# ScalarE and VectorE in program order through the whole attention part of a decoder layer, and other queues and turns for three of its steps

## The chip, the cores and the metric

The kernel runs on one core of one Trainium2 chip. The metric is device time in microseconds (us), the median of several runs of the same program; smaller is better. The profile is that of one execution. Engines go by the profile's names: PE multiplies matrices, DVE (VectorE) and ACT (ScalarE) do element-wise work, POOL and SP here mainly issue transfers. PSUM is the memory that PE writes; a 128x512 float32 tile of it is called a bank here.

## The reference, cut to what matters

One decoder layer for 512 tokens of width 1024, all in float32:

```python
h = RMSNorm(x);  z = h @ w_in            # one projection, cut into the parts below
A  = retention(rq, rk, rv)               # 4 heads, group norm, silu(rg) gate, @ w_ret_out
for (window, dilation) in (128,1), (512,4), (2048,16):   # 3 head groups, 4 heads of 128 each
    q, k = rotate(RMSNorm(aq)), rotate(RMSNorm(ak))
    s = q k^T / sqrt(128), masked;  m = max(s);  e = exp(s - m);  l = sum(e)
    o_g = (e / l) v;  lse_g = m + log(l)
Bt = sum_g softmax_g(lse_g) * o_g        # groups merged by their denominators, @ w_att_out
x  = x + (sig(gA) * A' + sig(gB) * Bt') @ w_o
x  = x + relu(RMSNorm(x) @ w_up)^2 @ w_down
x  = x + sig(RMSNorm(x) @ w_pg) * (p @ w_pp)
```

The change lies in the three groups of the attention. With 512 tokens, group 0 has four blocks of 128 queries, three of them with 256 keys; groups 1 and 2 have four blocks of 128 queries and 128 keys each, groups 1 and 2 being gathered by residue classes of the token number.

## The kernel before, in words

**Products.** Every product of two float32 matrices is made of three matmuls of a shorter type: each operand is split into a high part and the rest. For a weight, a piece of 128x1024 is loaded (`raw`, L212, by SP), ACT writes its high part (`whi`, L250), DVE the rest (`wlo`, L251), and `mm3` (L262 to L264) issues three matmuls on PE. `whi` and `wlo` have four buffers each, `raw` six. Units of weights are fetched and split two ahead of their use (`ahead`, `units`).

**Seven products.** The projections of the values, of the retention's keys and a few more are made by `seven_products`, which saves one of eight block products: sums of loaded weights are made by DVE (`raw<-raw,raw`, L226) or on the way in by POOL's accumulating DMA (L228). Its results leave PSUM by `after` in `values_seven`: products 1, 3, 4 and 5 by ACT's copy (L757), 2, 6 and 7 by DVE (L759, L761), which adds the bank to what stands in SBUF (`m`, `v`). A bank (`pg`, `pa`, `sc`, `pe`, `ph`, `po`, `pc` are its names) takes the next product only once it was read.

**Attention.** `att_proj` makes q or k of a group and rotates it (L575 to L580), with the norm's factor from POOL (L651) applied at L655; `scores` multiplies q and k to a bank `sc`, and `softmax` takes it: DVE adds the mask (`sm`, L678), takes the maximum (`mx`, L681) and the bias (`st`, L682, L684), ACT takes the exponential and its sum (`se`, L687). `turn` transposes the exponentials on PE (`pe`, L694), `weigh_values` multiplies them with the values (`po`, L835). `rescale` merges a group with those before it: factors `f`, `w`, `inv` (L863 to L871), for the last group the scaling of its sixteen exponential tiles by ACT (`se`, L876), `wide` (L878) and its transposition on PE (`pc`, L884), through DRAM to all partitions (L887, L892) and onto the output `oT` (L897).

**Order.** The Python program writes instructions in one order: a product, and between its pieces what stands in a queue of deferred steps (`later(lag, ...)` at the end, `prompt(lag, ...)` at the front; a lag is counted in pieces, `tick`; `force` runs the queue until a named step is done). A scheduler then fixes the order on each engine and may move instructions ahead of one another. Inside `manual_schedule(engines=...)` the named engines keep the written order. Before the change that held in the attention for the first two projections only (L703); outside it the scheduler chose.

Of the kernel before, what the change touches and what calls it, by code (L numbers as in the profile page):

```python
# [11 lines left out]
F32 = mybir.dt.float32  # L12
# [5 lines left out]
P = 128  # L18
S = 512
D = 1024  # L20
NT = S // P
# [3 lines left out]
H = 4  # L25
HD = 128
NG = 3
DIL = 4
# [51 lines left out]
class Block:  # L80
# [618 lines left out]
    def attention(self):  # L699

        nc = self.nc
        with self.tc.manual_schedule(engines={nc.scalar.engine, nc.vector.engine}):
            qk = self.att_proj(0, 0), self.att_proj(0, 1)  # L703
        nc.sync.dma_start(self.mask, self.a["c_mask"])
        self.gain_rows(1, NG)
        self.rot_rows(1)
        self.spare = True
        self.left = self.token_factors_seven()
        rq = self.rq
        qk1 = self.att_proj(1, 0), self.att_proj(1, 1)  # L710
        pT = [self.big("pT") for _ in range(2)]
        first, turned = self.scores(0, *qk, rq, None, pT)
        strided = self.const.tile([P, NT, 2, H], F32, name="st0p")
        self.prompt(10, lambda: self.to_strided(first, strided))
        past, turned1 = self.scores(1, *qk1, self.rq, strided, None, 18)
        self.later(24, lambda: self.rescale(1, strided, past), ("past", 1))
        v0, v1 = self.values_seven((self.r, self.r_minus))
        for g, v, pTs, lag in ((0, v0, turned, 2), (1, v1, turned1, 8)):
            values = self.weigh_values(g, v, pTs)
            for r in range(NT):  # L720
                self.later(lag, lambda r=r, values=values: values(r), ("att", g, r))
        qk = self.att_proj(2, 0), self.att_proj(2, 1)
        last, turned = self.scores(2, *qk, self.rq, past, None, 14)
        self.later(21, lambda: self.rescale(2, past, last), ("past", 2))
        dec, kdec = self.decays()
        kd, v2 = self.values_seven((None, self.r_minus), self.ret_keys(kdec))
        values = self.weigh_values(2, v2, turned)
        for r in range(NT):
            self.later(5, lambda r=r, values=values: values(r), ("att", 2, r))
        return dec, kd  # L730

    def values_seven(self, scale, ready=None):

        nc = self.nc
        for j in range(2):
            self.force(("S", j))
        held, out = {}, {}

        def tile(n):
            if n not in out:  # L740
                out[n] = self.big("v")
            return out[n]

        def after(m, p, ps):
            t = p if m in (1, 2, 3, 6) else 2 + p
            main = m in (1, 2, 4)
            r = scale[0 if main else 1]
            by = {} if r is None else dict(scale=r[:, t : t + 1])
            if main:
                o = tile(0)[:, t]  # L750
            elif m in (3, 5):
                o = self.tmp("m3") if m == 3 else self.tabp.tile([P, 512], F32, tag="tab", name=self.nm("m5"))
                held[{3: 6, 5: 7}[m], p] = o
            else:
                o = held.pop((m, p))
            if m in (1, 3, 5, 4):
                nc.scalar.activation(o, ps, AF.Copy, **by)  # L757
            elif r is None:
                nc.vector.tensor_tensor(o, o, ps, op=ALU.add)  # L759
            else:  # L760
                nc.vector.scalar_tensor_tensor(o, ps, r[:, t : t + 1], o, op0=ALU.mult, op1=ALU.add)  # L761
            if m in (6, 7):
                for q in range(DIL):
                    nc.sync.dma_start(tile(1)[32 * t : 32 * (t + 1), q], o[q : P : DIL])
            if m in (2, 4) and ready is not None:
                ready(t, o)

        self.seven_products(self.left, after)
        return tile(0), tile(1)

    def scores(self, g, qT, kT, rq, past, held=None, lag=2):

        nc = self.nc
        st = self.const.tile([P, NT, 2, H], F32, name=f"st{g}")
        pTs = [[] for _ in range(NT)]
        self.es = {}
        slots = None if held is None else [b[:, i] for b in held for i in range(4)]

        def block(r):
            m, l = st[:, r, 0], st[:, r, 1]  # L780
            rs = slice(r * P, (r + 1) * P)
            es = []
            wide = g == 0 and r > 0
            if not wide:
                sc = self.bank("sc")
                for h in range(H):
                    nc.tensor.matmul(sc[:, h * P : (h + 1) * P], qT[:, h, rs], kT[:, h, rs], start=True, stop=True)  # L787
                es.append(self.softmax(sc, P, H, self.mask[:, 128 * (g + 1) : 128 * (g + 2)], rq[:, r], m, l,
                                       None if past is None else past[:, r, 0]))
                self.es[g, r] = es[0]  # L790
            else:
                for hp in range(2):
                    sc = self.bank("sc")
                    for h in range(2):
                        nc.tensor.matmul(sc[:, h * 256 : (h + 1) * 256], qT[:, 2 * hp + h, rs],
                                         kT[:, 2 * hp + h, (r - 1) * P : (r + 1) * P], start=True, stop=True)
                    hs = slice(2 * hp, 2 * hp + 2)
                    es.append(self.softmax(sc, 256, 2, self.mask[:, 0:256], rq[:, r, hs], m[:, hs], l[:, hs]))
            for e in es:
                self.later((5, 8, 11)[g], lambda e=e: turn(e, r), ("pT", g, r))  # L800

        def turn(e, r):
            if g == 2:
                self.force(("past", 2))
            if g == 1 and not self.pT1:
                self.pT1.append(self.big("pT"))
            out = slots.pop(0) if slots else self.pT1[0][:, r] if g == 1 else None
            pTs[r].append(self.transpose4(e, out))

        for r in range(NT):  # L810
            self.later(lag, lambda r=r: block(r), ("sc", g, r))
        return st, pTs
# [43 lines left out]
    def rescale(self, g, past, st):  # L856
# [25 lines left out]
        def turn():  # L882
            ps = self.bank("pc")
            nc.tensor.transpose(ps[: H * NT, :P], wide, self.ident)  # L884
            turned = self.turned[: H * NT]
            nc.scalar.activation(turned, ps[: H * NT, :P], AF.Copy)
            nc.scalar.dma_start(d.rearrange("a (r l) -> (a r) l", r=DIL), turned)  # L887
# [4 lines left out]
                nc.scalar.dma_start(spread[0][:, h], d[h : h + 1].to_broadcast([P, S]))  # L892

        def scale():
            for h in range(H):
                o = self.oT[0][:, h]
                nc.vector.tensor_tensor(o, o, spread[0][:, h], op=ALU.mult)  # L897
# [619 lines left out]
```

## Time and profile before

| | before |
|---|---|
| runs | 954.59, 952.70, 952.63 us |
| median | 952.7 us |
| the profiled execution, time | 955.36 us |
| its span on the core | 953.6 us, so 1.8 us lie around it |
| mean granted PE clock | 0.997 |
| PE busy | 943.3 us, 99% of the span |
| DVE busy | 718.4 us, 75% |
| ACT busy | 562.1 us, 59% |
| POOL busy | 159.5 us, 17% |

The attention part lies between about 70 and 270 us of the span: the first group's softmaxes at 105 to 119 us, the second's at 135 to 146 us, the third's at 239 to 250 us. In rows of the profile, `out<-in` names the tiles that an instruction writes and reads; a time in brackets at a row's end is how long the engine idled before it, and for whom. Matmuls of PE overlap, so the time between two starts, not a row's duration, is what one costs.

### The profile page before, as it was taken

Reading aid. Unit: us, or ns where it says so; the run is one execution under the profiler, and the core shown is the slowest. Engines: PE = TensorE matmul, PEld = TensorE weight load, DVE = VectorE, ACT = ScalarE, POOL = GpSimd, SP = SyncE. Lnnn points to the kernel's source line nnn. Section 1 sums busy time; section 2 is a strip of 40 time slices with the busy share of each in tenths; the row PEclk is TensorE's granted clock in tenths of the full one; section 3 lists DMA queues with packets and bytes.
Section 4 is the critical chain, followed back from the end, with each engine's and each line's share of the span. In section 5 each row is a group of like instructions: output and inputs, shape, how many; then the busy total and the mean of one; then the engine's idle time right before and its main releaser. Section 6 shows DMA issues by size and latency. Waiting matters only on the chain.

```text
span 953.6 us, 14325 instructions
## 1 busy us (share of the span) xinstructions
PE 943.3 (99%) x5357; PEld 826.2 (87%) x5357; DVE 718.4 (75%) x997; ACT 562.1 (59%) x1065; POOL 159.5 (17%) x140
## 2 busy tenths in 40 slices
PE   9999999999899999999999999999999999999998
PEld 6888888888788888999988888988998998998887
DVE  7789964766697849386937889799499689769953
ACT  5657775445745566576714446884494486467651
POOL 0322210222001112223012211111212302112100
PEclk9999999999999999999999999999999999999999
DMA  9953466258437645869737677868958968876911
GB/s 333 282 170 82 106 141 215 64 118 195 148 111 155 173 100 138 163 181 217 232 115 236 148 178 214 206 153 222 199 156 202 191 183 157 224 172 159 288 50 56
DMA packets 92549, 162.87 MB, mean 171 GB/s; under 512 B 8608, under 2 KB 20544, under 8 KB 92480
## 3 DMA queue, kind: packets, MB, share of 16 engines
q1 hardware_dynamic: 65168, 113.37, 36.4%
q0 software_dynamic: 23936, 46.14, 29.0%
q10 hardware_dynamic: 3376, 2.44, 0.9%
q8 instruction: 42, 0.69, 0.3%
q14 instruction: 27, 0.22, 0.1%
HBM read 153.49 MB, written 6.34 MB: 168 GB/s over the span
## 4 chain that ended last, share of the span: by engine, by line
PE 92%; DVE 3%; ACT 1%; issue 1%; DMA 1%; POOL 1%; SPq 0%; ACTq 0%; POOLq 0%; DVEq 0%
PE pg L264 25%; PE pg L262 25%; PE pg L263 25%; PE pa L264 3%; PE pa L263 3%; PE pa L262 3%; PE po L835 1%; PE ph L590 1%; DVE wlo L251 1%; PE pe L694 1%; PE sc L787 1%; PE ry L1083 1%; PE kv L1070 1%; PE ry L1085 1%; DVE ro L578 0%
## 5 line engine op out<-in xcount | busy, mean ns | idle before, releaser
L251 DVE TENSOR_TENSOR wlo<-raw,whi 128x1024 fp32r<-128x1024 f32 (+1 forms) x258 | 306.8, 1198 | 112.7 <-ACT whi L250 111.8
L250 ACT ACTIVATE whi<-raw 128x1024 fp32r<-128x1024 f32 (+1 forms) x257 | 266.3, 1041 | 212.1 <-PE pg L264 87.2
L263 PE MATMUL pg<-f,whi 128*128 128x256 f32 x384 | 108.7, 283 | 0.0
L264 PE MATMUL pg<-f,wlo 128*128 128x256 f32 x384 | 108.7, 283 | 0.0
L262 PE MATMUL pg<-f,whi 128*128 128x256 f32 x384 | 108.7, 283 | 0.0
L262 PE MATMUL pg<-whi,hh 128*128 128x512 f32 x248 | 98.6, 398 | 0.0
L264 PE MATMUL pg<-whi,hl 128*128 128x512 f32 x248 | 97.1, 392 | 0.0
L263 PE MATMUL pg<-wlo,hh 128*128 128x512 f32 x248 | 96.8, 390 | 0.0
L262 PE MATMUL pg<-whi,f 128*128 128x512 f32 x192 | 75.4, 393 | 0.0
L263 PE MATMUL pg<-wlo,f 128*128 128x512 f32 x192 | 74.8, 389 | 0.0
L264 PE MATMUL pg<-whi,f 128*128 128x512 f32 x192 | 74.8, 389 | 0.0
L262 PEld LDWEIGHTS pg<-f,whi 128*128 128x128 f32 x384 | 73.7, 192 | 0.2
L263 PEld LDWEIGHTS pg<-f,whi 128*128 128x128 f32 x384 | 73.7, 192 | 0.2
L264 PEld LDWEIGHTS pg<-f,wlo 128*128 128x128 f32 x384 | 73.7, 192 | 0.0
L228 POOL DMA_DIRECT2D raw<-in_w_in x32 | 38.9, 1216 | 197.8 <-DVE wlo L251 193.0
L264 PEld LDWEIGHTS pg<-whi,hl 128*128 128x128 f32 x248 | 46.6, 188 | 9.8
L263 PEld LDWEIGHTS pg<-wlo,hh 128*128 128x128 f32 x248 | 46.6, 188 | 9.2
L262 PEld LDWEIGHTS pg<-whi,hh 128*128 128x128 f32 x248 | 46.6, 188 | 9.2
L228 POOL DMA_DIRECT2D raw<-in_w_down x24 | 29.0, 1215 | 139.3 <-DVE wlo L251 108.2
L262 PE MATMUL pg<-whi,us 128*128 128x512 f32 x128 | 52.1, 407 | 0.0
L228 POOL DMA_DIRECT2D raw<-in_w_up x24 | 29.0, 1211 | 135.0 <-DVE wlo L251 124.7
L264 PE MATMUL pg<-whi,us 128*128 128x512 f32 x128 | 50.0, 391 | 0.0
(280 smaller groups left out, 2298.0 us busy)
## 6 DMA issues: line engine op xcount, KB each, us to landing
raw<-in_w_in SPq DMA_DIRECT2D x72, 512.0 KB, 4.1
raw<-in_w_in POOLq DMA_DIRECT2D x32, 512.0 KB, 6.2
raw<-in_w_up SPq DMA_DIRECT2D x32, 512.0 KB, 4.6
raw<-in_w_down SPq DMA_DIRECT2D x32, 512.0 KB, 4.6
raw<-in_w_up POOLq DMA_DIRECT2D x24, 512.0 KB, 6.6
raw<-in_w_down POOLq DMA_DIRECT2D x24, 512.0 KB, 5.9
x<-in_x SPq DMA_DIRECT2D x8, 512.0 KB, 8.2
raw<-in_w_ret_out SPq DMA_DIRECT2D x8, 512.0 KB, 3.8
```

The lines of the kernel that those rows point to most:

```text
L228: self.nc.gpsimd.dma_start(raw, self.chained[i].rearrange("(k p) n -> p k n", p=P), accum_op=ALU.add)
L250: self.pin(nc.scalar.activation(R(hi[:, i]), raw[:, i], AF.Copy))
L251: nc.vector.tensor_tensor(R(lo[:, i]), raw[:, i], hi[:, i], op=ALU.subtract)
L262: t.matmul(ps, sh, mh, start=first, stop=False, skip_group_check=more)
L263: t.matmul(ps, sh, ml, start=False, stop=False, skip_group_check=more)
L264: t.matmul(ps, sl, mh, start=False, stop=last, skip_group_check=more)
L590: self.nc.tensor.transpose(ps[:, t * P : (t + 1) * P], rots[t][:, h * HD : (h + 1) * HD], self.ident)
L694: self.nc.tensor.transpose(ps[:, k * P : (k + 1) * P], e[:, k * P : (k + 1) * P], self.ident)
L787: nc.tensor.matmul(sc[:, h * P : (h + 1) * P], qT[:, h, rs], kT[:, h, rs], start=True, stop=True)
L835: nc.tensor.matmul(po[:, h * P : (h + 1) * P], v[:, vt, h * HD : (h + 1) * HD], pt, start=b == 0, stop=b == len(blocks) - 1)
L1070: nc.tensor.matmul(ps, kd[:, n, hs], v[:, n, c], start=True, stop=True)
L1083: nc.tensor.matmul(y, sT[0][:, r], v[:, i, c], start=True, stop=i == 0)
```

## The change

Four edits, and nothing in what is computed:

1. `manual_schedule` for ACT and DVE now holds to the end of `attention`: both engines run everything of it in the order in which the program writes it.
2. Each of the eight value tiles that are regrouped by residue class was moved by four DMAs of 64 KB on SP's queue; it is now one DMA of 256 KB on ACT's queue, two pieces later.
3. The first group's scores are due 4 pieces after they are put in the queue, not 2; the last group's exponentials are transposed 15 pieces after, not 11.
4. The scaling of `oT` runs the queue until the last step of the group before has been done.

```diff
         with self.tc.manual_schedule(engines={nc.scalar.engine, nc.vector.engine}):
             qk = self.att_proj(0, 0), self.att_proj(0, 1)
-        nc.sync.dma_start(self.mask, self.a["c_mask"])
...
-        first, turned = self.scores(0, *qk, rq, None, pT)
...
-        return dec, kd
+            nc.sync.dma_start(self.mask, self.a["c_mask"])
...
+            first, turned = self.scores(0, *qk, rq, None, pT, 4)
...
+                self.later(5, lambda r=r, values=values: values(r), ("att", 2, r))
         return dec, kd
@@ values_seven
             if m in (6, 7):
-                for q in range(DIL):
-                    nc.sync.dma_start(tile(1)[32 * t : 32 * (t + 1), q], o[q : P : DIL])
+                rows = tile(1)[32 * t : 32 * (t + 1)]
+                self.prompt(2, lambda: nc.scalar.dma_start(rows, o))
@@ scores
             for e in es:
-                self.later((5, 8, 11)[g], lambda e=e: turn(e, r), ("pT", g, r))
+                self.later((5, 8, 15)[g], lambda e=e: turn(e, r), ("pT", g, r))
@@ rescale
         def scale():
+            self.force(("att", g - 1, NT - 1))
             for h in range(H):
                 o = self.oT[0][:, h]
                 nc.vector.tensor_tensor(o, o, spread[0][:, h], op=ALU.mult)
```

What it moves shows at two places above all. In the rows below, numbers behind a name tell one tile from another; the same tile has other numbers in the two kernels.

**The first group's softmaxes, DVE.** Before:

```order
L655 TENSOR_TENSOR ro_1067<-ro_1067,r_1059 128x512
L655 TENSOR_TENSOR ro_1109<-ro_1109,r_1101 128x512
L678 TENSOR_TENSOR sm_1152<-sc_1147,mg_110 128x512
L251 TENSOR_TENSOR wlo_1185<-raw_1130,whi_1184 128x1024
L681 TENSOR_REDUCE mx_1155<-sm_1152 128x4
L251 TENSOR_TENSOR wlo_1250<-raw_1247,whi_1249 128x1024
L682 SCALAR_TENSOR_TENSOR st_1121<-mx_1155,rq_144 128x4
L678 TENSOR_TENSOR sm_1165<-sc_1162,mg_110 128x512
L251 TENSOR_TENSOR wlo_1271<-raw_1268,whi_1270 128x1024
L681 TENSOR_REDUCE mx_1168<-sm_1165 128x2
L682 SCALAR_TENSOR_TENSOR st_1121<-mx_1168,rq_144 128x2
L678 TENSOR_TENSOR sm_1176<-sc_1173,mg_110 128x512
```

and now:

```order
L655 TENSOR_TENSOR ro_1108<-ro_1108,r_1100 128x512
L251 TENSOR_TENSOR wlo_1126<-raw_1123,whi_1125 128x1024
L226 TENSOR_TENSOR raw_1129<-raw_1129,raw_1123 128x1024
L251 TENSOR_TENSOR wlo_1147<-raw_1129,whi_1146 128x1024
L678 TENSOR_TENSOR sm_1170<-sc_1165,mg_110 128x512
L681 TENSOR_REDUCE mx_1173<-sm_1170 128x4
L682 SCALAR_TENSOR_TENSOR st_1120<-mx_1173,rq_144 128x4
L678 TENSOR_TENSOR sm_1183<-sc_1180,mg_110 128x512
L681 TENSOR_REDUCE mx_1186<-sm_1183 128x2
L682 SCALAR_TENSOR_TENSOR st_1120<-mx_1186,rq_144 128x2
L678 TENSOR_TENSOR sm_1194<-sc_1191,mg_110 128x512
L681 TENSOR_REDUCE mx_1197<-sm_1194 128x2
```

Two `wlo` that stood between the steps of the first two softmaxes now stand ahead of them, and with them the addition of two loaded weights (L226); behind the third softmax the engine takes no further one before it has done `wlo_1205`:

```order
L682 SCALAR_TENSOR_TENSOR st_1120<-mx_1197,rq_144 128x2
L251 TENSOR_TENSOR wlo_1205<-raw_1202,whi_1204 128x1024
L678 TENSOR_TENSOR sm_1226<-sc_1223,mg_110 128x512
L681 TENSOR_REDUCE mx_1229<-sm_1226 128x2
L682 SCALAR_TENSOR_TENSOR st_1120<-mx_1229,rq_144 128x2
L678 TENSOR_TENSOR sm_1237<-sc_1234,mg_110 128x512
```

**The same stretch, ACT.** Before:

```order
L250 ACTIVATE whi_1126<-raw_1124 128x1024
L624 ACTIVATE j_1102,ss_1099<-pg_946 128x128 x4
L250 ACTIVATE whi_1184<-raw_1130 128x1024
L250 ACTIVATE whi_1249<-raw_1247 128x1024
L250 ACTIVATE whi_1270<-raw_1268 128x1024
L687 ACTIVATE se_1153,st_1121<-sm_1152,st_1121,rq_144 128x128 x4
L687 ACTIVATE se_1166,st_1121<-sm_1165,st_1121,rq_144 128x256 x2
L757 ACTIVATE v_1259<-pg_1133,r 128x512
L687 ACTIVATE se_1177,st_1121<-sm_1176,st_1121,rq_144 128x256 x2
L757 ACTIVATE v_1259<-pg_1140,r 128x512
L687 ACTIVATE se_1207,st_1121<-sm_1206,st_1121,rq_144 128x256 x2
L757 ACTIVATE m_1281<-pg_1189,r_more 128x512
```

and now:

```order
L250 ACTIVATE whi_1146<-raw_1129 128x1024
L687 ACTIVATE se_1171,st_1120<-sm_1170,st_1120,rq_144 128x128 x4
L687 ACTIVATE se_1184,st_1120<-sm_1183,st_1120,rq_144 128x256 x2
L687 ACTIVATE se_1195,st_1120<-sm_1194,st_1120,rq_144 128x256 x2
L250 ACTIVATE whi_1204<-raw_1202 128x1024
L757 ACTIVATE v_1214<-pg_1132,r 128x512
L757 ACTIVATE v_1214<-pg_1139,r 128x512
L687 ACTIVATE se_1227,st_1120<-sm_1226,st_1120,rq_144 128x256 x2
L687 ACTIVATE se_1238,st_1120<-sm_1237,st_1120,rq_144 128x256 x2
L687 ACTIVATE se_1249,st_1120<-sm_1248,st_1120,rq_144 128x256 x2
L687 ACTIVATE se_1260,st_1120<-sm_1259,st_1120,rq_144 128x256 x2
L250 ACTIVATE whi_1269<-raw_1267 128x1024
```

Before, all four `whi` were written ahead of the first exponential; now `whi_1204` stands behind three blocks of exponentials and `whi_1269` behind four more.

**The last group's softmaxes, ACT.** Before:

```order
L250 ACTIVATE whi_2382<-raw_2226 128x1024
L250 ACTIVATE whi_2441<-raw_2249 128x1024
L687 ACTIVATE se_2356,st_2159<-sm_2355,st_2159,rqs_1928 128x128 x4
L250 ACTIVATE whi_2459<-raw_2006 128x1024
L687 ACTIVATE se_2372,st_2159<-sm_2371,st_2159,rqs_1928 128x128 x4
L250 ACTIVATE whi_2463<-raw_2169 128x1024
L687 ACTIVATE se_2415,st_2159<-sm_2414,st_2159,rqs_1928 128x128 x4
L250 ACTIVATE whi_2557<-raw_2555 128x1024
L250 ACTIVATE whi_2563<-raw_2561 128x1024
L687 ACTIVATE se_2431,st_2159<-sm_2430,st_2159,rqs_1928 128x128 x4
L864 ACTIVATE f_2484<-f_2484 128x16
```

and now:

```order
L687 ACTIVATE se_2343,st_2146<-sm_2342,st_2146,rqs_1915 128x128 x4
L687 ACTIVATE se_2359,st_2146<-sm_2358,st_2146,rqs_1915 128x128 x4
L250 ACTIVATE whi_2369<-raw_2213 128x1024
L764 DMA v_2380<-m_2297 32x4x512
L687 ACTIVATE se_2395,st_2146<-sm_2394,st_2146,rqs_1915 128x128 x4
L250 ACTIVATE whi_2405<-raw_2236 128x1024
L764 DMA v_2380<-m_2305 32x4x512
L687 ACTIVATE se_2430,st_2146<-sm_2429,st_2146,rqs_1915 128x128 x4
L250 ACTIVATE whi_2440<-raw_1993 128x1024
L250 ACTIVATE whi_2444<-raw_2156 128x1024
L864 ACTIVATE f_2461<-f_2461 128x16
L876 ACTIVATE se_2343<-se_2343,inv_2467 128x128 x4
```

Before, `whi` stood ahead of the exponentials or between them two or three blocks early; now each stands behind the exponentials of the block written before it, and the last two `whi` behind the last block's.

**The last group's softmaxes and factors, DVE.** Before:

```order
L761 SCALAR_TENSOR_TENSOR m_2247<-pg_2179,r_more,m_2247 128x512
L684 TENSOR_TENSOR st_2159<-st_2159,st_1123 128x4
L251 TENSOR_TENSOR wlo_2564<-raw_2561,whi_2563 128x1024
L863 TENSOR_TENSOR f_2484<-st_2159,st_1123 128x16
L226 TENSOR_TENSOR raw_2755<-raw_2755,raw_2749 128x1024
L866 TENSOR_TENSOR w_2487<-f_2484,st_1123 128x16
L867 TENSOR_TENSOR st_2159<-st_2159,w_2487 128x4x4
L870 RECIPROCAL inv_2490<-st_2159 128x16
L871 TENSOR_TENSOR f_2484<-f_2484,inv_2490 128x16
L878 COPY wide_2509<-f_2484 128x4x4
L575 TENSOR_TENSOR ro_2517<-rz_2512,rotc_109 128x512
L578 TENSOR_TENSOR ro_2518<-rz_2512,rotc_109 128x4x64 x2
```

and now the end of the softmaxes:

```order
L678 TENSOR_TENSOR sm_2429<-sc_2424,mg_110 128x512
L681 TENSOR_REDUCE mx_2432<-sm_2429 128x4
L682 SCALAR_TENSOR_TENSOR st_2146<-mx_2432,rqs_1915 128x4
L684 TENSOR_TENSOR st_2146<-st_2146,st_1122 128x4
L251 TENSOR_TENSOR wlo_2441<-raw_1993,whi_2440 128x1024
L251 TENSOR_TENSOR wlo_2445<-raw_2156,whi_2444 128x1024
L761 SCALAR_TENSOR_TENSOR m_2226<-pg_2159,r_more,m_2226 128x512
L863 TENSOR_TENSOR f_2461<-st_2146,st_1122 128x16
```

and, after the factors:

```order
L878 COPY wide_2486<-f_2461 128x4x4
L226 TENSOR_TENSOR raw_2713<-raw_2713,raw_2707 128x1024
L575 TENSOR_TENSOR ro_2494<-rz_2489,rotc_109 128x512
L578 TENSOR_TENSOR ro_2495<-rz_2489,rotc_109 128x4x64 x2
L580 TENSOR_TENSOR v_2204<-ro_2494,ro_2495 128x512
L761 SCALAR_TENSOR_TENSOR m_2234<-pg_2166,r_more,m_2234 128x512
```

Before, `m_2247` (L761) stood between the last softmax's steps, and a weight addition (L226) ahead of the factors; now `m_2226` stands behind both last `wlo`, the factors come before the weight addition, and `m_2234` stands behind the rotation of `rz_2489`, which ACT writes after its sixteen scalings (L876).

On PE the written order of the products is nearly kept, with 4982 rows in place of 4985; on POOL nothing moves; SP loses the thirty-two small DMAs of the value tiles, and two of its loads stand two places earlier. Lines from L893 on have one number more than before.

More of the change, by code (lines that the diff above doesn't have):

```diff
@@ L703, in attention @@
             qk = self.att_proj(0, 0), self.att_proj(0, 1)
-        nc.sync.dma_start(self.mask, self.a["c_mask"])
[L705 to L711, printed above, removed]
-        first, turned = self.scores(0, *qk, rq, None, pT)
-        strided = self.const.tile([P, NT, 2, H], F32, name="st0p")
@@ L714, in attention @@
[L714 to L719, printed above, removed]
-            for r in range(NT):
-                self.later(lag, lambda r=r, values=values: values(r), ("att", g, r))
@@ L722, in attention @@
[L722 to L729, printed above, removed]
+            nc.sync.dma_start(self.mask, self.a["c_mask"])
@@ new lines, in attention @@
+            self.gain_rows(1, NG)
+            self.rot_rows(1)
+            self.spare = True
+            self.left = self.token_factors_seven()
+            rq = self.rq
+            qk1 = self.att_proj(1, 0), self.att_proj(1, 1)
+            pT = [self.big("pT") for _ in range(2)]
+            first, turned = self.scores(0, *qk, rq, None, pT, 4)
+            strided = self.const.tile([P, NT, 2, H], F32, name="st0p")
+            self.prompt(10, lambda: self.to_strided(first, strided))
+            past, turned1 = self.scores(1, *qk1, self.rq, strided, None, 18)
@@ new lines, in attention @@
+            self.later(24, lambda: self.rescale(1, strided, past), ("past", 1))
+            v0, v1 = self.values_seven((self.r, self.r_minus))
+            for g, v, pTs, lag in ((0, v0, turned, 2), (1, v1, turned1, 8)):
+                values = self.weigh_values(g, v, pTs)
+                for r in range(NT):
+                    self.later(lag, lambda r=r, values=values: values(r), ("att", g, r))
+            qk = self.att_proj(2, 0), self.att_proj(2, 1)
+            last, turned = self.scores(2, *qk, self.rq, past, None, 14)
@@ L730, in attention @@
+            self.later(21, lambda: self.rescale(2, past, last), ("past", 2))
+            dec, kdec = self.decays()
+            kd, v2 = self.values_seven((None, self.r_minus), self.ret_keys(kdec))
+            values = self.weigh_values(2, v2, turned)
+            for r in range(NT):
+                self.later(5, lambda r=r, values=values: values(r), ("att", 2, r))
         return dec, kd
```

## The prediction

> **What bounds the kernel now.** I read the busy times first, then the chain of work that ended last, then PE's waits, then PE's busy time by windows of the attention part.
>
> ```profile
> PE 943.3 (99%) x5357; PEld 826.2 (87%) x5357; DVE 718.4 (75%) x997; ACT 562.1 (59%) x1065; POOL 159.5 (17%) x140
> PE 92%; DVE 3%; ACT 1%; issue 1%; DMA 1%; POOL 1%; SPq 0%; ACTq 0%; POOLq 0%; DVEq 0%
> PE pc L884 <- DVE wide L878: 3.0, 1, 3.0
> PE sc L795 <- DVE sm L678: 0.8, 1, 0.8
> ```
>
> PE sets the end: busy for 943.3 of 953.6 us. The change removes no matmul, so it can only win PE's gaps, and any new gap is added to the time in full. In the attention there are two gaps: 0.8 us, where scores wait for a bank that a softmax must read, and 3.0 us, where the transposition `pc` waits for `wide`. The windows (us, then the busy times of PE, PEld, DVE, ACT, POOL, then the granted clock) show the second gap's after-effect:
>
> ```profile
> 96.00:120.00 24.00, 23.18 (x112) 19.29 (x111) 21.92 (x42) 17.13 (x50) 6.38 (x5) 1.00 0.46 100
> 240.00:264.00 24.00, 20.98 (x95) 16.94 (x94) 15.35 (x29) 19.10 (x57) 0.00 (x0) 0.93 0.41 133
> 254.00:256.00 2.00, 0.00 (x0) 0.00 (x0) 1.82 (x6) 0.37 (x2) 0.00 (x0) 0.97 0.30 74
> 256.00:258.00 2.00, 1.89 (x8) 1.56 (x8) 0.00 (x0) 2.00 (x9) 0.00 (x0) 0.50 0.93 352
> 258.00:260.00 2.00, 2.00 (x10) 1.53 (x10) 0.00 (x0) 2.00 (x8) 0.00 (x0) 0.67 0.35 135
> ```
>
> After the 3.0 us the clock is 0.50, then 0.67: half speed for 2 x 0.50/0.50 + 2 x 0.33/0.50 = 3.3 us, which loses 1.65 us of PE's work. So the old gaps are worth 0.8 + 3.0 + 1.65 = 5.5 us; that is the most that the change can win.
>
> The chain in order of time says why `wide` was late:
>
> ```profile
> 250.19 1.61 SPq L764
> 251.85 1.90 DMA v<-m
> 253.75 1.21 DVE raw L226
> 254.96 0.10 DVE w L866
> 255.78 0.19 DVE wide L878
> 256.11 0.37 PE pc L884
> ```
>
> ```profile
> 253.73 1.22 DVE L226 TENSOR_TENSOR raw<-raw,raw 128x1024 f32<-128x1024 f32 x1 [2.79 <-DMA v<-m]
> ```
>
> A weight addition (L226), ahead of the factors on DVE, stood 2.79 us for a transfer behind the small value-tile DMAs on SP's queue, and the factors behind it.
>
> **The change part by part.** The value-tile DMAs and the order of the factors answer that gap: SP no longer issues them, and `wide` stands ahead of the addition. Gain: 3.0 + 1.65 = 4.65. The issues move to ACT, eight of them; the nearest row of ACT's queue is 0.33 us, the longest of SP's above 1.61, so 2.6 to 12.9 us of ACT's queue in all, of which four lie on the chains below. I take nothing, since the row on the same queue says 0.3 each; the upper end, 4 x 1.3 = 5, goes into the range.
>
> ```profile
> 262.27 0.33 ACTq L892 DMA_DIRECT2D fb<-f_dram  x1
> ```
>
> [...] The longer turns (4 for 2, 15 for 11) and the forced step move matmuls among others of the same count; their cover is PE's other products, and I cost them at nothing.
>
> The program order is the large part. DVE's and ACT's work does not change, but the weight splits that PE needs next now stand behind exponentials and softmaxes. What one step costs, DVE first:
>
> ```profile
> 104.54 0.69 DVE L655 TENSOR_TENSOR ro<-ro,r 128x512 f32<-128x512 f32 x1 [0.30 <-POOL r L651]
> 105.15 0.68 DVE L678 TENSOR_TENSOR sm<-sc,mg 128x512 f32<-128x512 f32 x1
> 105.75 1.22 DVE L251 TENSOR_TENSOR wlo<-raw,whi 128x1024 fp32r<-128x1024 f32 x1
> 106.88 0.68 DVE L681 TENSOR_REDUCE mx<-sm 128x4 f32<-128x512 f32 x1
> 111.21 0.68 DVE L678 TENSOR_TENSOR sm<-sc,mg 128x512 f32<-128x512 f32 x1
> 112.72 0.68 DVE L678 TENSOR_TENSOR sm<-sc,mg 128x512 f32<-128x512 f32 x1
> 246.10 0.74 DVE L761 SCALAR_TENSOR_TENSOR m<-pg,r_more,m 128x512 f32<-128x512 f32 x1
> 246.76 0.67 DVE L681 TENSOR_REDUCE mx<-sm 128x4 f32<-128x512 f32 x1
> 260.74 0.69 DVE L575 TENSOR_TENSOR ro<-rz,rotc 128x512 f32<-128x512 f32 x1 [4.78 <-ACT rz L987]
> 261.35 0.75 DVE L578 TENSOR_TENSOR ro<-rz,rotc 128x256 f32<-128x256 f32 x2
> 262.02 1.22 DVE L226 TENSOR_TENSOR raw<-raw,raw 128x1024 f32<-128x1024 f32 x1
> ```
>
> By the distance of starts: `wlo` 1.13 (the addition, of the same shape, too), a softmax `sm`, `mx`, `st` 1.51 (1.6 with the second `st`), one 128x512 step 0.61, `m` 0.66, the two `ro` halves 0.67. ACT, and PE:
>
> ```profile
> 106.68 1.06 ACT L250 ACTIVATE whi<-raw 128x1024 fp32r<-128x1024 f32 x1 [4.30 <-PE pg L264]
> 108.80 0.49 ACT L687 ACTIVATE se<-sm,st,rq 128x128 f32<-128x128 f32 x1 [1.07 <-DVE st L682]
> 110.25 0.48 ACT L687 ACTIVATE se<-sm,st,rq 128x128 f32<-128x128 f32 x1
> 113.08 0.59 ACT L687 ACTIVATE se<-sm,st,rq 128x256 f32<-128x256 f32 x1
> 114.25 0.67 ACT L757 ACTIVATE v<-pg,r 128x512 f32<-128x512 f32 x1
> 255.63 4.79 ACT L876 ACTIVATE se<-se,inv 128x128 f32<-128x128 f32 x16 [2.86 <-DVE inv L870]
> 261.27 1.28 ACT L987 ACTIVATE rz<-v,dec 128x128 f32<-128x128 f32 x4
> 98.40 0.39 PE L262 MATMUL pg<-whi,hh 128*128 128x512 f32 x1
> 101.12 1.05 PE L787 MATMUL sc<-hT,hT 128*128 128x128 f32 x8
> 233.24 1.95 PE L787 MATMUL sc<-hT,hT 128*128 128x128 f32 x16
> 234.94 0.48 PE L262 MATMUL pg<-whi,us 128*128 128x512 f32 x1
> ```
>
> `whi` 1.06; a block of four small exponentials 1.93 (three steps take 1.45); one of two wide ones 1.17; sixteen scalings 4.79; four `rz` 1.28. Twelve matmuls of 128x512 lie between 98.40 and 101.12, 0.227 each; a block of scores is a quarter of 234.94 - 233.24, 0.43, and four transpositions, of the same shape, are put at the same.
>
> *First group.* DVE applies the norm when POOL's factor comes, at 104.54, to 105.15. Then by the order written: `wlo` 1.13, the addition 1.13, `whi` of the sum on ACT 1.06, its `wlo` 1.13: the first softmax starts at 109.6, not at 105.15. Its bias is there at 111.1; three blocks of exponentials, 1.93 + 2 x 1.17, end at 115.4; `whi` to 116.45, `wlo` to 117.6. Four softmaxes, 4 x 1.51, end at 123.6, the last exponentials at 124.8, `whi` at 125.9, `wlo` at 127.0. PE, from 101.12 to the matmul that reads that `wlo`, has 62 matmuls, 7 blocks of scores and 2 of transpositions: 14.1 + 3.0 + 0.9 = 18.0, so it could be there at 119.1. It loses 7.9, of which 0.8 was lost before: +7.1. Some 3 us of it come where PE wants the `wlo` of 117.6 and a bank that the next softmax frees at 118.2 (PE's work before is 48 matmuls and the 7 blocks of scores, 13.9, to 115.0), the rest behind.
>
> *Second group.* PE may take the product that follows its last scores and transpositions only when `m` (L761) has emptied a bank, and that `m` stands on DVE behind a pair of `wlo`, whose `whi` stand on ACT behind the second block of exponentials. From the first block of scores: softmax 1.6, exponentials 1.93, `whi` 1.06, `wlo` 1.13, two `m` or `v` 1.32, softmax 1.6, exponentials 1.93, two `whi` 2.12, the second `wlo` 1.13, `m` 0.66: 14.5. By the written order PE has 36 matmuls, 3 blocks of scores, 2 of transpositions until then, 8.2 + 1.3 + 0.9 = 10.4: it waits 4.1. The next `m` stands behind two softmaxes, 3.2 + 0.66, against 12 matmuls, 2.7: 1.1 more. +5.2.
>
> *Third group.* The same, longer: softmax 1.6, two blocks of exponentials 3.86, `whi` 1.06, `wlo` 1.13, two `m` 1.32, softmax 1.6, exponentials 1.93, `whi` 1.06, `wlo` 1.13, two additions of `v` 1.22, softmax 1.6, exponentials 1.93, two `whi` 2.12, `wlo` 1.13, `m` 0.66: 23.3, against 48 matmuls and 3 blocks of scores, 10.9 + 1.3 = 12.2: +11.1. Then the second `m` stands behind the factors (0.8 between the end of the addition at 254.96 and `wide` at 255.78, put at 0.9 with `f`), sixteen scalings 4.79, `rz` 1.28 and `ro` 1.9, with its own 0.66: 9.5, against 12 matmuls, `pc` and twelve transpositions, 4.2: +5.3.
>
> *Clock.* Each gap of over 3 us is followed by 1.65 of loss; where PE soon waits again for the same chain, that is hidden. I count it after the last gap of the first and of the third group: +3.3. [...]
>
> **Sum:** 7.1 + 5.2 + 11.1 + 5.3 + 3.3 - 4.65 = +27.3 us. On the profiled execution's own 955.4 that is 982.7; its 955.36 lies 2.7 above the median of 952.7, so I forecast 952.7 + 27.3, about **980 us**.
>
> **The rivals.**
> *A, the splits come in time.* DVE idles long in the same stretches (4.78 above, before `ro`), so volume leaves room. If PE's cover were as long as the chains, only the old gaps would go: 952.7 - 5.5 = 947.2. Against it: the chains are by 4 to 11 us longer than their cover, and each of them alternates between two engines.
> *B, one or two of the three stretches hold.* The chains start when scores come; if half of the blocks are ready earlier than I let them start, or a product's bank is free sooner, the third group's 11.1 and the first's 7.1 shrink by half, and their clock loss of 3.3 goes: 952.7 + 27.3 - 9.1 - 3.3 = 967.6; with the second group's gone too, 962.
> *C, worse.* The weight addition, now behind the factors but still ahead of `m`, waited 2.79 us before; if its load is as late again, that is added to the last chain, and four ACT issues at 1.61 add 5: 980 + 8 = 988; with a slow clock after every gap, 2 x 1.65, about 991. For it: loads depend on buffers freed later by late splits. Against it: SP has fewer issues ahead.
> *D, no change:* gaps new and old cancel within 2 us. Nothing in the order says so.
>
> **How the numbers follow.** Forecast 0.60 (972 to 986); A 0.06; B 0.17; C 0.14; D 0.03, of which most lies within 0.2% (1.9 us, about what a measurement of this kernel can tell from no change). Range 962 to 991. Faster 0.06, same 0.03, slower 0.91.
>
> **What would show it.** PE idle of some 8 us between 113 and 127 us, with `whi` or `sm` as what it waited for; of some 5 in the second group, of some 16 in the third, with DVE's `m` at L761 as releaser; no wait of `pc` for `wide` behind a transfer; in the lines of `whi`, idle time released by DVE's `st`; clock of 0.5 after each long gap. If PE's idle time in the attention stays below 10 us, the walk is wrong; if PE waits for DMA instead, rival C.

## The result, and the profile after

The changed kernel takes 989.7 us in the median of four runs (986.7 to 993.2), the kernel before 952.7: a ratio of 1.0388, with a 95% interval of 1.0364 to 1.0412. The forecast was 980, with 972 to 986 as its likeliest part and 962 to 991 as its range; 989.7 lies in the range, near its upper end. The profiled execution took 990.4 us, its span is 988.6, 35.0 longer than that of before.

The page of the changed kernel, its first rows, the busy times and the chain by engines:

```profile
PE 954.5 (97%) x5357; PEld 831.6 (84%) x5357; DVE 722.2 (73%) x997; ACT 561.1 (57%) x1065; POOL 156.8 (16%) x140
...
PE 77%; DVE 12%; ACT 4%; issue 3%; DMA 3%; POOL 0%; ACTq 0%; SPq 0%; DVEq 0%; POOLq 0%
```

PE is busy for 11.2 us more (954.5 for 943.3) with the same 5357 matmuls, and idle for 34.1 us in place of 10.3: 23.8 more. The 35.0 us are idle time and longer matmuls; the mean granted clock is 0.988, where it was 0.997. On the chain that ended last PE has 77% in place of 92%, DVE 12% in place of 3%.

The timeline of PE in the attention, its rows with a wait; in brackets the wait and for whom:

```profile
119.52 0.76 PE L262 MATMUL pa<-whi,hh 128*128 128x512 f32 x1 [3.65 <-DVE sm L678]
...
127.78 1.10 PE L262 MATMUL pg<-whi,us 128*128 128x512 f32 x2 [3.09 <-ACT m L757]
...
159.44 0.47 PE L262 MATMUL pg<-whi,hh 128*128 128x512 f32 x1 [4.02 <-DVE m L761]
...
232.29 0.50 PE L263 MATMUL pg<-wlo,hh 128*128 128x512 f32 x1 [1.05 <-DVE wlo L251]
...
260.44 0.47 PE L262 MATMUL pg<-whi,us 128*128 128x512 f32 x1 [0.68 <-DVE m L761]
...
265.72 1.22 PE L262 MATMUL pg<-whi,us 128*128 128x512 f32 x2 [2.27 <-ACT whi L250]
...
276.03 0.77 PE L262 MATMUL pg<-whi,hh 128*128 128x512 f32 x1 [5.51 <-DVE f L863]
...
280.52 1.47 PE L694 MATMUL pe<-ident,se 128*128 128x128 f32 x12
285.81 0.50 PE L262 MATMUL pg<-whi,hh 128*128 128x512 f32 x1 [3.82 <-DVE m L761]
...
321.63 0.50 PE L262 MATMUL pg<-whi,us 128*128 128x512 f32 x1 [1.28 <-DVE ro L1007]
```

These are the places that were forecast: two in the first group (3.65 for a bank that a softmax frees, 3.09 for a bank that ACT's copy `m` frees behind `whi`), one of 4.02 in the second for DVE's `m`, and in the third 0.68, 2.27 and 5.51 ahead of the last product (the 5.51 is put down to `f`, the instruction behind `m` on DVE), then 3.82 for the second `m`. Not forecast are 1.05 at 232 us and 1.28 at 322 us. The old wait of `pc` for `wide` is gone: `pc` and the transpositions at 280.5 run without one. PE's windows of 2 us behind four of these waits show the clock (the third number from the right):

```profile
120.00:122.00 2.00, 2.00 (x6) 1.53 (x5) 1.90 (x6) 1.38 (x5) 0.00 (x0) 0.50 0.77 248
...
130.00:132.00 2.00, 2.00 (x6) 1.55 (x5) 1.74 (x2) 1.17 (x2) 1.19 (x1) 0.50 0.61 73
...
266.00:268.00 2.00, 1.96 (x5) 1.05 (x6) 2.00 (x3) 0.00 (x0) 0.00 (x0) 0.50 0.01 3
...
276.00:278.00 2.00, 1.97 (x5) 1.61 (x6) 0.96 (x5) 1.20 (x5) 0.00 (x0) 0.50 0.96 340
```

The chain in order of time, between the third group's last two blocks of scores and the last product, shows the mechanism step by step:

```profile
263.76 0.95 ACT se L687 x4
264.72 0.95 ACT whi L250
...
265.69 1.23 DVE wlo L251
266.92 1.19 DVE v L759 x2
268.12 0.61 DVE sm L678
...
270.27 1.62 ACT se L687 x7
271.88 0.95 ACT whi L250
...
274.01 1.22 DVE wlo L251
275.22 0.66 DVE m L761
```

Exponentials (0.95 is their last part), `whi`, `wlo`, two additions, the next softmax, its exponentials, two `whi`, the second `wlo`, then `m`, and only at 276.03 the matmul: ACT and DVE alternate, each waiting for the other, and PE waits for both.

Two instructions do the same work in both kernels and show how much was lost where: the last squares of the third group's projections (`j`, the second time in its row), which lie behind the first two groups, and the first product of the retention (`kv`), behind the attention. Before:

```profile
L624 ACT ACTIVATE j<-pg x96: 253/277/377, 19.7 to 210.8; 128x128 f32<-128x128 f32 x96
...
L1070 PE MATMUL kv<-v,v x24: 377/378/382, 328.7 to 400.1; 128*128 128x256 f32 x24
```

and after:

```profile
L624 ACT ACTIVATE j<-pg x96: 257/278/392, 19.4 to 226.2; 128x128 f32<-128x128 f32 x96
...
L1071 PE MATMUL kv<-v,v x24: 377/378/382, 361.2 to 432.6; 128*128 128x256 f32 x24
```

Up to the last `j` the change lost 226.2 - 210.8 = 15.4 us; from there to the first `kv` 135.0 - 117.9 = 17.1; from there to the end of the span 627.4 - 624.9 = 2.5.

### The profile page after: what moved, and what is told of

Its sections match the earlier page's. It is cut to its first block, busy times and chain, and to the rows that moved or that the text cites. A ratio compares the mean times of both kernels' runs of the same rounds, so it can differ in the third digit from the quotient of the medians.

```text
span 988.6 us, 14273 instructions
## 1 busy us (share of the span) xinstructions
PE 954.5 (97%) x5357; PEld 831.6 (84%) x5357; DVE 722.2 (73%) x997; ACT 561.1 (57%) x1065; POOL 156.8 (16%) x140
## 4 chain that ended last, share of the span: by engine, by line
PE 77%; DVE 12%; ACT 4%; issue 3%; DMA 3%; POOL 0%; ACTq 0%; SPq 0%; DVEq 0%; POOLq 0%
PE pg L262 21%; PE pg L263 21%; PE pg L264 21%; DVE wlo L251 3%; PE pa L262 2%; PE pa L264 2%; PE pa L263 2%; ACT se L687 2%; ACT whi L250 1%; DMA raw<-in_w_in 1%; DMA raw<-in_w_down 1%; PE po L835 1%; PE ph L590 1%; DVE ro L578 1%; DVE raw L226 1%
## 5 line engine op out<-in xcount | busy, mean ns | idle before, releaser
L262 PEld LDWEIGHTS pg<-whi,hh 128*128 128x128 f32 x248 | 47.8, 193 | 23.8 <-issue 10.1
L262 PE MATMUL pg<-whi,us 128*128 128x512 f32 x128 | 53.6, 423 | 7.4 <-ACT m L757 3.1
L263 PE MATMUL pg<-wlo,us 128*128 128x512 f32 x128 | 51.6, 403 | 0.3 <-DVE wlo L251 0.3
L226 DVE TENSOR_TENSOR raw<-raw,raw 128x1024 f32<-128x1024 f32 x32 | 39.0, 1220 | 17.4 <-DMA raw<-in_w_in 10.3
```

The costliest lines, as they stand in the source:

```text
L226: self.nc.vector.tensor_tensor(total, total, part, op=ALU.add)
L262: t.matmul(ps, sh, mh, start=first, stop=False, skip_group_check=more)
L263: t.matmul(ps, sh, ml, start=False, stop=False, skip_group_check=more)
```

## The experiments

All ratios are to the kernel before, in the same job on the same chip; its medians there lay between 952.7 and 955.8 us, so the ratios compare better than the times.

| kernel | median, us | ratio | 95% interval |
|---|---|---|---|
| the change | 989.7 | 1.0388 | 1.0364 to 1.0412 |
| program order alone | 988.1 | 1.0370 | 1.0354 to 1.0385 |
| the rest, no program order | 964.0 | 1.0113 | 1.0096 to 1.0130 |
| DMA edit and forced step alone | 962.7 | 1.0101 | 1.0078 to 1.0124 |
| lags and forced step alone | 954.0 | 1.0001 | 0.9988 to 1.0014 |
| change, order on DVE alone | 974.7 | 1.0229 | 1.0207 to 1.0251 |
| change, order on ACT alone | 973.8 | 1.0190 | 1.0175 to 1.0205 |
| change, order in groups 0 and 1 | 980.3 | 1.0261 | 1.0240 to 1.0282 |
| change, order in group 2 | 975.8 | 1.0207 | 1.0190 to 1.0224 |
| change, splits three units ahead | 989.5 | 1.0356 | 1.0341 to 1.0372 |
| change, idle matmuls in four waits | 990.3 | 1.0373 | 1.0355 to 1.0392 |
| before, value tiles on POOL's queue | 954.3 | 1.0006 | 0.9994 to 1.0019 |
| before, value tiles in one DMA on SP | 956.1 | 1.0023 | 1.0008 to 1.0038 |

**Program order alone, and the rest alone.** The first undoes edits 2 to 4, the second edit 1:

```diff
# program order alone: against the change
-                rows = tile(1)[32 * t : 32 * (t + 1)]
-                self.prompt(2, lambda: nc.scalar.dma_start(rows, o))
+                for q in range(DIL):
+                    nc.sync.dma_start(tile(1)[32 * t : 32 * (t + 1), q], o[q : P : DIL])
-            first, turned = self.scores(0, *qk, rq, None, pT, 4)
+            first, turned = self.scores(0, *qk, rq, None, pT)
-                self.later((5, 8, 15)[g], lambda e=e: turn(e, r), ("pT", g, r))
+                self.later((5, 8, 11)[g], lambda e=e: turn(e, r), ("pT", g, r))
-            self.force(("att", g - 1, NT - 1))
# the rest: manual_schedule ends behind the first two projections, as before
```

> Program order alone: the change's first edit, with the value-tile DMAs on SP's queue, the lags of 2 and 11 and no forced step, as before. Theory (weight splits stand behind exponentials and softmaxes): nearly the whole loss stays, 985 to 996 us, with PE waiting for DVE's m (L761), for softmaxes and for whi in all three groups. Rival (the moved DMAs or the later turns cause the loss): 955 to 970 us.

> The other three edits without program order: one DMA per value tile on ACT's queue, the lags of 4 and 15, the forced step; the scheduler orders ACT and DVE as before. Theory: no loss, and the old wait of pc for wide (3.0 us and 1.65 us of slow clock) can go: 947 to 953 us. Rival (DMAs on ACT's queue hold up exponentials): 965 us or more.

Program order alone costs 3.7%, as much as the whole change, so the time of the first expectation held. Of the waits that it named, only those for `whi` are large, 10.0 us in all; those for `m` are 1.2 and for a softmax 0.3. PE waits there for banks that ACT's copies of transposed tiles free:

```profile
PE pe L694 <- ACT pT L158: 5.2, 1, 5.2
...
PE pe L694 <- ACT turned L886: 3.3, 1, 3.3
```

Up to the last `j` this run loses 18.4 us, and 13.1 from there to the first `kv`, where the change loses 15.4 and 17.1. That program order costs this much without the other edits is shown; that both times are so nearly equal is in part a coincidence, since the other edits, within the written order, move the waits. What each of them does there was not run by itself.

The second expectation did not hold: without program order the other edits still cost 1.1%, where no loss was expected. PE waits twice for `whi` in that kernel:

```profile
250.67 0.73 PE L262 MATMUL pg<-whi,hh 128*128 128x512 f32 x2 [2.83 <-ACT whi L250]
...
263.10 0.50 PE L262 MATMUL pg<-hh,whi 128*128 128x512 f32 x1 [2.95 <-ACT whi L250]
```

and ACT's timeline shows where these `whi` stand:

```profile
249.10 0.48 ACT L687 ACTIVATE se<-sm,st,rqs 128x128 f32<-128x128 f32 x1
...
249.57 1.04 ACT L250 ACTIVATE whi<-raw 128x1024 fp32r<-128x1024 f32 x1
...
260.84 1.26 ACT L988 ACTIVATE rz<-v,dec 128x128 f32<-128x128 f32 x4
...
262.01 1.99 ACT L250 ACTIVATE whi<-raw 128x1024 fp32r<-128x1024 f32 x2
```

The first stands behind the third block's exponentials, the second behind the last block's, the sixteen scalings and `rz`. Before, all `whi` for these products stood ahead of the last block's exponentials. It is the mechanism of the change, a weight split behind other work of ACT, and here the scheduler put the splits there.

**Which of the other edits.** The DMA edit with the forced step (without that step the DMA edit gives no program, since the scaling of `oT` would be written ahead of the first `oT`), and the two lags with the forced step, each on the kernel before.

```diff
# DMA alone: against before
-                for q in range(DIL):
-                    nc.sync.dma_start(tile(1)[32 * t : 32 * (t + 1), q], o[q : P : DIL])
+                rows = tile(1)[32 * t : 32 * (t + 1)]
+                self.prompt(2, lambda: nc.scalar.dma_start(rows, o))
+            self.force(("att", g - 1, NT - 1))
# lags alone: against before
-        first, turned = self.scores(0, *qk, rq, None, pT)
+        first, turned = self.scores(0, *qk, rq, None, pT, 4)
-                self.later((5, 8, 11)[g], lambda e=e: turn(e, r), ("pT", g, r))
+                self.later((5, 8, 15)[g], lambda e=e: turn(e, r), ("pT", g, r))
+            self.force(("att", g - 1, NT - 1))
```

> The DMA edit with the forced step that it needs, on the kernel before: one DMA per value tile on ACT's queue, lags of 2 and 11, the scheduler's order. The scheduler then puts the last two whi of the last group behind exponentials again, as in the run without program order. Theory (a whi behind exponentials is the loss, whoever puts it there): 960 to 966 us, with PE waiting twice some 3 us for whi in the last group. Rival (the lags cause that run's loss): 948 to 955 us.

> The two lags (4 and 15) and the forced step alone, on the kernel before: value tiles by SP's small DMAs, the scheduler's order. Its order of whi and exponentials in the last group is that of before. Theory: 951 to 955 us, no change. Rival (the lags cause the loss of the run without program order): 960 to 966 us.

Both came out by the theory: 1.0101 and 1.0001. PE's waits with the DMA edit alone:

```profile
PE pg L262 <- ACT whi L250: 4.9, 2, 2.8
```

So in the scheduler's order the lags cost nothing, and the DMA edit costs 1% by itself. That is not time that its issues take from ACT, as the rival of the run before had it: in the trace of that run, which has the same edit, an issue starts at 251.13 and takes 0.55 us, and the exponentials around it start at 250.52, 251.00, 251.47 and 251.95, 0.47 to 0.48 us apart; in the block before, without an issue, they start 0.48 to 0.49 apart. What moved is the scheduler's order of `whi`. Why the scheduler answers so was not tried.

The run with the lags alone shows one thing more. Its order of DVE around the factors and its transfers on SP are those of before, and yet the old wait of `pc` is 1.36 us in its trace, not 3.0:

```profile
254.33 0.27 PE L884 MATMUL pc<-ident,wide 128*16 128x128 f32 x1 [1.36 <-DVE wide L878]
```

```profile
240.00:264.00 24.00, 22.64 (x107) 18.50 (x106) 17.00 (x32) 20.66 (x61) 0.00 (x0) 1.00 0.47 149
```

The clock stays at 1.00, and the profiled execution took 953.1 us, while its median over ten runs is that of before. The eight small DMAs that SP issues between 244 and 258 us land 5.4 us after their issue before, in the median, and 3.8 here, and the addition (L226) waits 2.79 us before and 1.13 here. So the 3.0 us that the prediction counted as the change's gain seem to have been long in the one execution that was profiled, which lay 2.7 us above its median; there is no second profile of the kernel before.

**One engine alone.**

```diff
# against the change; and the same with nc.scalar.engine alone
         with self.tc.manual_schedule(engines={nc.scalar.engine, nc.vector.engine}):
             qk = self.att_proj(0, 0), self.att_proj(0, 1)
+        with self.tc.manual_schedule(engines={nc.vector.engine}):
             nc.sync.dma_start(self.mask, self.a["c_mask"])
```

> The change with only DVE held in program order in the attention behind the first two projections; ACT is ordered by the scheduler. Theory: whi no longer has to stand behind exponentials, so the chains lose their ACT part, but m still stands behind wlo and wlo behind softmaxes: 955 to 970 us. Rival (DVE's order carries the loss alone): 983 to 992 us.

> The change with only ACT held in program order in the attention behind the first two projections; DVE is ordered by the scheduler. Theory: whi still stands behind the exponentials, 1.9 us a block, but DVE may take m and wlo ahead of softmaxes: 960 to 985 us, more than with DVE alone. Rival (DVE's order carries the loss alone): 950 to 956 us.

Each alone costs about 2%. With ACT the time lies in the expected range, but ACT was to cost more than DVE, and by the ratios it does not (1.0190 and 1.0229). With DVE the expectation was 5 us too low. PE's waits with DVE alone in order:

```profile
PE pg L262 <- ACT whi L250: 5.0, 2, 4.3
PE pg L263 <- DVE wlo L251: 4.0, 2, 2.5
```

Even with ACT free, PE waits 5.0 us for `whi`, 4.3 of them in the third group, where the scheduler, with the DMA edit in place, puts it behind the last exponentials and `rz`. Some 1% of either loss may thus be the DMA edit's; what these runs settle is that neither engine's order carries the whole.

**One part of the attention alone.**

```diff
# groups 0 and 1: against the change
-            qk = self.att_proj(2, 0), self.att_proj(2, 1)
+        qk = self.att_proj(2, 0), self.att_proj(2, 1)      # and all behind it
# group 2: the part ahead of this line is outside, a manual_schedule of both engines starts here
```

> The change with program order ending ahead of the last group's projections: groups 0 and 1 in order, group 2 by the scheduler. Theory (each group has its own chains): the waits of the first two groups stay, 3.6 + 3.1 + 4.0 us and their slow clock, those of the last group go: 962 to 972 us. Rival (one group carries nearly all): under 958 or over 980 us.

> The change with program order only from the last group's projections on: groups 0 and 1 by the scheduler. Theory: the last group's waits, 2.3 + 5.5 + 3.8 us and more, with slow clock, less the old wait of pc: 964 to 975 us, and with the run of groups 0 and 1 alone the differences to the kernel before add to those of the whole, 37 us, within 6. Rival: under 958 or over 980 us.

The first median, 980.3, lies above what was expected and just inside the rival's band, the second, 975.8, at the upper edge of what was expected. The two losses, 24.4 and 20.0 us against 955.8 in that job, add to 44, more than the change's 37 and past the margin of 6. The markers show why. With groups 0 and 1 in order the last `j` comes at 226.7 us, 15.9 late, about as much as in the whole change (15.4); from there to the first `kv` are 124.2 us, 6.3 over before, in the group that the scheduler orders. With group 2 in order the last `j` comes at 210.7, not late, and from there to `kv` are 136.7 us, 18.8 over. So each part has its own loss, as the theory says and against the rival, and some 6 us in the scheduled group are the DMA edit's, which the expectation had taken as harmless: the run with the DMA edit alone loses 6.0 in the same stretch.

**Splits earlier.**

```diff
# against the change
-        self.ahead(n + (0 if self.pinned else self.AHEAD))
+        self.ahead(max(n, min(4, n + (0 if self.pinned else self.AHEAD))))
+        self.AHEAD = 3        # at the start of attention; 2 again at its end
```

> The change with weights split three units ahead in the attention, not two (never more than the four buffers hold). Theory: each whi and wlo is written up to one unit, 12 matmuls or 2.7 us, earlier in both engines' order, so PE's waits shrink by up to that much each: 970 to 984 us. Rival (PE waits for banks that m or a softmax frees, not for splits): 986 to 993 us.

The rival holds: 989.5 us. The ratio is 0.003 lower than the change's, 3 us, which is at the edge of what the intervals tell, and far from the 6 to 20 us that were expected. PE's waits, of the change and then with the earlier splits:

```profile
PE pg L262 <- DVE m L761: 8.5, 3, 4.0
PE pg L262 <- DVE f L863: 5.5, 1, 5.5
...
PE pg L262 <- ACT whi L250: 2.3, 1, 2.3
PE pg L262 <- DVE r L1326: 2.0, 3, 1.0
```

```profile
PE pg L262 <- DVE f L865: 8.8, 1, 8.8
PE pg L262 <- DVE m L763: 7.2, 4, 2.9
PE pa L262 <- DVE sm L678: 4.1, 1, 4.1
PE pg L262 <- ACT m L759: 2.5, 1, 2.5
...
PE pa L262 <- ACT whi L250: 0.2, 1, 0.2
```

The waits for `whi` fall from 2.3 us to 0.2, those at banks that a softmax or `m` frees take their place (one of 8.8 at the last product). So the splits alone are not what counts: `m`, which frees a bank, stands behind whatever DVE was given first, and a `whi` or `wlo` taken earlier is more that stands ahead of it.

**Does a slow clock cost time?** The change, with matmuls that compute nothing wanted ahead of four waits:

```diff
# against the change, in seven_products
+    FILL = {76: 30, 133: 16, 136: 50, 138: 38}      # by the count of pieces
...
+                n = self.FILL.get(self.clock, 0)
+                if n:
+                    zb, zp = self.ident.bitcast(mybir.dt.bfloat16), banks["c", 0][:, :256]
+                    for _ in range(n):
+                        self.tc.keep_in_program_order(self.nc.tensor.matmul(zp, zb[:, :P], zb[:, :256], start=True, stop=True))
```

> The change with idle matmuls (identity times identity, into a bank that nobody reads then) ahead of four of PE's waits, 0.11 us each: 30 ahead of the second group's 4.0 us, 16, 50 and 38 ahead of the last group's 2.3, 5.5 and 3.8 us. They add nothing to what is computed and should keep PE's clock at full there. Theory (slow matmuls behind a wait are hidden where the next wait is set by the same chain on ACT and DVE): only the second group's slow stretch and the one behind the 3.8 us count, so 3.3 us less than the change, and the waits behind the other two grow by what is won. Rival (every slow stretch adds to the time): 6 to 7 us less.

The mean clock rose from 0.988 to 0.995, and the ratio is 1.0373 for 1.0388: too close to tell 3.3 us from none by the time, but not the rival's 6 to 7. The trace tells more. PE's timeline there, with the idle matmuls:

```profile
261.63 0.47 PE L263 MATMUL pg<-whi,us 128*128 128x512 f32 x1 [0.68 <-DVE m L762]
...
263.10 1.92 PE L1268 MATMUL pg<-ident 128*128 128x256 bf16 x16
...
270.59 5.63 PE L1268 MATMUL pg<-ident 128*128 128x256 bf16 x50
277.23 0.47 PE L263 MATMUL pg<-whi,hh 128*128 128x512 f32 x1 [1.01 <-DVE f L864]
...
280.18 4.31 PE L1268 MATMUL pg<-ident 128*128 128x256 bf16 x38
...
287.01 0.50 PE L263 MATMUL pg<-whi,hh 128*128 128x512 f32 x1 [1.21 <-DVE m L762]
```

From the product at 261.63 to the one at 277.23 are 15.60 us, and 9.78 from there to the one at 287.01. In the change the same three start at 260.44, 276.03 and 285.81: 15.59 and 9.78. With PE kept busy and at full clock (1.00 in each window of 4 us from 264 to 292, where the change has 0.56 to 0.86 in all but one) nothing comes sooner; ACT and DVE set these times, and the slow matmuls behind those waits were hidden, as the theory says. The waits behind the idle matmuls are shorter only because those fill them.

The two stretches that the theory did count, 3.3 us, gave less. From the end of the second group's wait to the product at 260.44 the change takes 101.00 us and this run 100.51; from the product at 285.81 to the first `kv`, at 361.2, they take 75.4 and 74.4 (in this run from 287.01 to 361.4). That is 0.5 and 1.0 us; a part of the rest went into other waits: that for `ro` (L1007, here L1008) is 1.8 in place of 1.3. The two spans (988.6 and 988.5) do not show this, since the profiled execution with idle matmuls was 2.1 us behind the other at the first group's wait already, ahead of all idle matmuls.

**Two ways to take the old wait away.** On the kernel before:

```diff
-                for q in range(DIL):
-                    nc.sync.dma_start(tile(1)[32 * t : 32 * (t + 1), q], o[q : P : DIL])
+                nc.gpsimd.dma_start(tile(1)[32 * t : 32 * (t + 1)], o)      # or nc.sync
```

> The kernel before with one DMA per value tile on POOL's queue, at the place where the four small ones stood. ACT's and DVE's order in the last group is that of before. Theory (the loads of the added weights wait for the value-tile transfers on SP's queue, and the factors behind them): the 3.0 us wait of pc and its slow clock go, 946.5 to 949.5 us. Rival (the loads are late by themselves): 952 to 954 us.

> The kernel before with one DMA of 256 KB per value tile on SP's queue in place of four of 64 KB: the same bytes on the same queue, a quarter of the issues. Theory (the issues of the small DMAs hold up SP's queue, up to 1.61 us each): the wait of pc shrinks, 947 to 951 us. Rival (the bytes on the queue, not the issues, make the loads late): 952 to 954 us.

Neither beats the kernel before: 1.0006 and 1.0023. On POOL's queue the wait of `pc` is 1.06 us, little under the 1.36 of the run with the lags alone, whose small DMAs stand on SP; with one DMA on SP it is 1.41. The addition (L226) still waits for its own load there, 0.83 us with POOL's queue and 1.17 with one DMA on SP. So the loads are late mostly by themselves, and the rival is the nearer in both, though the times lie above its 952 to 954. No run beat the kernel before.

## Why the prediction was right, step by step

The direction, the mechanism and the places were right, and 989.7 lies in the range, though above the 972 to 986 that the forecast held likeliest. The profiled execution took 990.4 us where the sum gave 982.7; the 7.7 that are missing lie in these steps.

*First and second group*, "+7.1", "+5.2" and 1.65 of clock: 14.0 in all, measured 15.4 up to the last `j`. The first group's last wait ended at 127.78, the walk had 127.0. The second group's second wait, 1.1, did not come; a slow stretch behind the first one did.

*A block of scores*, "0.43": misread. The sixteen matmuls of that row, 1.70 us, are two blocks and not four: the trace has 72 such matmuls for the nine blocks with 128 keys. A block takes 0.85, and with that PE's cover in the walk is longer by 3.0, 1.3 and 1.3 us in the three groups, and the sum is about 21.7 and not 27.3. The chains were longer than walked as well: from the first softmax to the product behind `m` 15.3 us in the second group, where the walk had 14.5, and 24.4 in the third, where it had 23.3. So it is partly luck that the waits came as near as they did; what made up for the 3.0 us in the first group was not followed.

*Third group*, "+11.1", "+5.3", 1.65 of clock, less 4.65: 13.4, measured 17.1. The first chain took 24.4 us, from the softmax at 251.66 to the product at 276.03, where the walk had 23.3; the second chain took 9.78, where it had 9.5. What the walk lacked were two more waits, 1.05 for a `wlo` in the products ahead of the third group's scores and 1.28 at 322 us, behind the attention's end, for DVE's rotations (L1007). They were not walked, since the walk began at each group's softmaxes.

*Behind the attention*, nothing: measured 2.5. Its rows are three waits for `r` (L1326) in the MLP, 2.0 us together, shown above among the change's waits; they stand in several of the experiments' traces too, between 0.3 and 2.0 us. What moves them stays open.

*Clock*, "+3.3", with the stretches behind other waits taken as hidden: the idle matmuls bore that out to 0.01 us in the third group. A part of PE's 11.2 us of more busy time is thus no loss, since it stands where PE would have idled. PE idles 23.0 us in the waits that were walked, and the walk had 29.5; twelve slow matmuls behind each of the 3.65, 2.27 and 5.51 take about 5.0 us more than at full clock and make up most of the difference. Of the stretches that were counted as a loss, 1.65 each, the last one of the third group cost 1.0 by the idle matmuls; the first group's was not filled.

*The old wait*, "-4.65": it is right for the profiled execution, which had it. For the median it was counted twice: the forecast took it off and also started from a median 2.7 us below that execution, and another trace with the same order has a wait of 1.36 and no slow clock. The two further runs speak against the 5.5 us that were to be won at most: with most of the wait gone, the times show no gain.

*The DMA edit*, "I take nothing": the issues on ACT's queue take 0.55 to 0.67 us each in the trace after, not 0.33, but exponentials that run across one keep their distance of 0.48 or 0.49. That they cost nothing in the written order is not shown by the times, since there the edit was undone only together with the lags. As the price of the edit with the scheduler's order, "nothing" was wrong: it costs 1% there.

*The rivals.* A, splits in time, fell, and the waits for `whi` and `m` show where. B fell as well: the waits of all three groups came, and even with half of the attention or one engine set free the times were 974 to 980, above its 962 to 968. D fell with the ratio. C gave the time that was measured, 988 to 991, but not its cause: the weight addition was late again, but DVE's timeline after shows that behind it DVE still waited for `rz`,

```profile
279.99 1.23 DVE L226 TENSOR_TENSOR raw<-raw,raw 128x1024 f32<-128x1024 f32 x1 [2.64 <-DMA raw<-in_w_in]
283.00 0.69 DVE L575 TENSOR_TENSOR ro<-rz,rotc 128x512 f32<-128x512 f32 x1 [1.79 <-ACT rz L988]
```

so its 2.64 us lay beside ACT's sixteen scalings and cost nothing. The price of C was a coincidence.

## What to carry to other kernels

An engine that is half idle on average can still be the bound if two of them take turns in a fixed order, as DVE and ACT do here, busy for 73% and 57% of the span: add up the chain between the points where the busiest engine waits, over both engines, and set it against that engine's work between the same points. A gap in one profile is one execution's gap; before its length is counted as a gain, a second trace or the median should bear it out. And an edit to a queue can cost more by what the scheduler then does with the order than by the transfer itself (here 1%, with an issue of 0.55 us beside which the exponentials keep their distance), so the order of the instructions is to be compared after each edit, small ones too.

## What was not expected of the hardware

The clock fell to half behind waits that are shorter than the 3.0 us in the profile before: behind 2.27 us, up to 265.72 us in the change, it is 0.50 in the next window, 266 to 268; behind 2.83 us in the run without program order the matmuls start 0.43 us apart, where those ahead of that wait start 0.23 apart. In the run with the lags alone it stayed at 1.00 behind 1.36 us. So the "over 3 us" of the prediction is not a bound below which idle time is free here. These runs don't show whether idle time shortly before such a wait bears on it: before the 2.27 us PE had also idled 0.68 us, up to 260.44.
